# Product-key lookup and weight grids: eight heads per operation, four tokens per first one-hot, the weight in the second one-hot

## The chip, the cores and the metric

The kernel runs on one core of a Trainium2 chip. The metric is the device time of one execution in microseconds; three executions of the kernel before give a median of 4173.94 us (4171.84 to 4176.83). The engines are named as in the profile: PE is TensorE (PEld its weight loads), DVE is VectorE, ACT is ScalarE, POOL is GpSimd, SP is SyncE, which issues most DMAs.

## The reference, cut to what matters

Two transformer blocks follow each other on 256 tokens of 1024 features. The first has attention and a mixture of 32 experts (top 4, three 1024x1024 matrices for each expert). The second has two layers, each with a mixer and a PEER feed-forward part; it works on the 256 tokens and, in its first layer, on 256 context tokens as well. PEER is the part that the change touches:

```
def peer_ffn(h, w_q, sub_keys, u_tab, v_tab):
    # 8 heads, 2 x 128 sub-keys, top 16 per half -> 256 candidates -> top 16
    def one_block(xb):                                  # 128 tokens
        q = (xb @ w_q).reshape(128, 8, 2, 64)
        s = einsum('thpd,pkd->thpk', q, sub_keys)
        s1, i1 = top_k(s[:, :, 0], 16)
        s2, i2 = top_k(s[:, :, 1], 16)
        cand_s = s1[..., :, None] + s2[..., None, :]
        cand_i = i1[..., :, None] * 128 + i2[..., None, :]
        top_s, pos = top_k(cand_s, 16)                  # over the 256 candidates
        idx = take_along_axis(cand_i, pos)              # 0 .. 16383
        wts = softmax(top_s)
        act = gelu(einsum('thkd,td->thk', u_tab[idx], xb)) * wts
        return einsum('thk,thkd->td', act, v_tab[idx])
```

Each token thus picks 8 x 16 = 128 of 16384 experts, each with a weight.

## The kernel before

The kernel gathers nothing. For PEER it multiplies all 16384 rows of `u_tab` with the 256 tokens (**U**, L150 to L152, three products of high and low parts, into the banks `ps_u`), takes gelu, multiplies with a **grid** of weights (L880), and multiplies the result with all rows of `v_tab` (**V**, L897, L898, L900, into the banks `ps_a`). Both tables are read in chunks `wr` and split into `wh` (ACT, L117) and `wl` (DVE, L118). The grid holds for each token and each expert the sum of the weights that the token gives the expert: 128x128 numbers for a token, the two halves of the expert number being row and column.

PEER runs three times. Stage **B** is the context's, in layer 0; stage **A** the tokens' in layer 0; stage **C** the tokens' in layer 1. Each has a `peer_prep` that makes the grids and a `peer_pass` that makes U and V. In `peer_prep` there are two blocks of 128 tokens, and for each:

- `topk`: scores, top 16 and softmax. At its end stands the lookup (L746): for each of 8 heads and 16 picks one operation over the 50 candidates that can be among the top 16, with an accumulated sum, 128 in all. Then the numbers are split into two halves (L753 to L756), transposed together with the weights, and copied to `it` (L761, three rows of 128 tokens).
- `grid`: for each token a first one-hot `o1` on DVE (L788: iota equal to the first half, times the weight), a second one-hot `o2`, in one buffer for two tokens, and a matmul of the two (L789). Four tokens fill a bank of `ps_a`; ACT evicts it (L790) to `stg`, and 16 tokens are stored to DRAM (L792). Of eight `o2` buffers in a row POOL makes two (L778, `POOL_AT`); in the second block of tokens (`share` = 2) DVE makes four (L780); the others are ACT's, as the absolute difference (L782, one for each token) and then 1 minus it, clipped at zero, for both tokens at once (L784). So ACT makes six of eight in the first block of a stage, 48 in all, and two of eight in the second.

The order of instructions on each engine is fixed when the kernel is built, by a scheduler that keeps a timeline of its own with assumed durations: of the instructions whose inputs and buffers its timeline has ready it takes the next. How much of one stage stands between the instructions of another is so decided by assumed times. The buffers of each kind are counted: in stages A and C `o1` has 8 (one token each) and `o2` has 4 (two tokens each), in stage B they have 6 (`NB1`) and 3. A V cannot stand ahead of its stage's grids, while U can: in stages A and C the U of 40 pairs of chunks may run ahead.

Stage B is written as a filler of the first block's mixture of experts. The order interleaves it with that part's expert chunks, which are named by the matmuls of gate and up projection (L1055) and of down projection (L1089). I call eight rows of the order with them (16 matmuls in the trace, two loads `mo` of 1 MiB each) an expert chunk. A branch (`overflow`) is a barrier at 540 us of the trace; 192 expert chunks stand in all, 27 of them ahead of B's grids.

Of the kernel before, what the change touches and what calls it, by code (L numbers as in the profile page):

```python
# [10 lines left out]
F32 = mybir.dt.float32  # L11
# [3 lines left out]
AF = mybir.ActivationFunctionType  # L15
ALU = mybir.AluOpType
AX = mybir.AxisListType
# [3 lines left out]
P = 128  # L21
# [24 lines left out]
GP = 1  # L46
SPB = 4
PB = 8
NB1 = 6
POOL_AT = (1,5)  # L50
EL = (1, 3, 5, 7)
MOE_FIRST = 6
NCAND = sum(w for _, w in CAND) + 8
# [11 lines left out]
def kernel(ctx: ExitStack, tc: tile.TileContext, a: dict, out: bass.AP):  # L65
    nc = tc.nc
# [20 lines left out]
    def psum(tag):  # L87
        if tag == "g":
            tag = gtags[gnext[0] % len(gtags)]
            gnext[0] += 1  # L90
        return ps.tile([P, 512], F32, tag=tag, name="ps_" + tag, bufs=4 if tag == "a" else 2)
# [8 lines left out]
    ident, iota, lt_m, gt_m, ones_m = C("ident"), C("iota"), C("lt"), C("gt"), C("ones")  # L100
# [487 lines left out]
    for k2 in range(4):  # L588
        yb = ytr(k2)
        for c in range(2):  # L590
            k = 2 * k2 + c
# [105 lines left out]
    def topk(l, q, tk, idx, pt):  # L697
        keys, qT = q
        sc = []
        for tb in range(2):  # L700
# [39 lines left out]
            nc.vector.tensor_copy(tf, tx)  # L740
            ef = tk.tile([P, 8, 16], F32, tag="ef", name="ef")
            eqs = tk.tile([P, 8, 64], F32, tag="sc", name="eq", bufs=2)
            for h in range(8):
                for k in range(16):
                    eq = eqs[:, k % 8, 0:NCAND]
                    nc.vector.scalar_tensor_tensor(eq, iota[:, 0:NCAND], tf[:, h, k:k + 1], ce[:, h, :], op0=ALU.is_equal,  # L746
                                                   op1=ALU.mult, accum_out=ef[:, h, k:k + 1])
                if h % 2:
                    yield
            ei = tk.tile([P, P], I32, tag="ts", name="ei")  # L750
            e2 = tk.tile([P, P], I32, tag="tx", name="e2")
# [5 lines left out]
            tp = psum(pt)  # L757
            for i in range(3):
                nc.tensor.transpose(tp[:, i * P:(i + 1) * P], iw[i], ident)
            it = tk.tile([P, 3, P], F32, tag="it", name="it", bufs=2)  # L760
            nc.scalar.activation(it.rearrange("p c t -> p (c t)"), tp[:, :384], AF.Copy)  # L761
            idx.append(it)
            yield

    def grid(tk, it, gd, bufs, share):
        nstg, nb1, nb2 = bufs
        for tq in range(8):
            stg = tk.tile([P, P, 16], F32, tag="stg", name="stg", bufs=nstg)
            for t4 in range(4):
                bank = psum("a").rearrange("p (t i) -> p t i", t=4)  # L770
                for i2 in range(2):
                    o2q = tk.tile([P, 2, P], F32, tag="o2", name="o2", bufs=nb2)
                    on_pool = (2 * t4 + i2) in POOL_AT
                    on_dve = share and (2 * t4 + i2) % share == 0
                    for i in range(2):
                        t = tq * 16 + t4 * 4 + i2 * 2 + i
                        if on_pool:
                            nc.gpsimd.tensor_scalar(o2q[:, i, :], iota, it[:, 1, t:t + 1], None, op0=ALU.is_equal)  # L778
                        elif on_dve:
                            nc.vector.tensor_scalar(o2q[:, i, :], iota, it[:, 1, t:t + 1], None, op0=ALU.is_equal)  # L780
                        else:
                            nc.scalar.activation(o2q[:, i, :], iota, AF.Abs, bias=it[:, 1, t:t + 1], scale=-1.0)  # L782
                    if not on_dve and not on_pool:
                        nc.scalar.activation(o2q, o2q, AF.Relu, bias=1.0, scale=-1.0)  # L784
                    for i in range(2):
                        t = tq * 16 + t4 * 4 + i2 * 2 + i
                        o1 = tk.tile([P, P], F32, tag="o1", name="o1", bufs=nb1)
                        nc.vector.tensor_scalar(o1, iota, it[:, 0, t:t + 1], it[:, 2, t:t + 1], op0=ALU.is_equal, op1=ALU.mult)  # L788
                        nc.tensor.matmul(bank[:, 2 * i2 + i, :], o2q[:, i, :], o1, start=True, stop=True)  # L789
                nc.scalar.activation(stg[:, :, t4 * 4:t4 * 4 + 4].rearrange("p i t -> p t i"), bank, AF.Copy)  # L790
                yield
            STQ.dma_start(gd[:, tq], stg)  # L792

    def peer_prep(l, xm, tk, gd, bufs=(3, 8, 4), pt="g"):
        keys = tk.tile([P, P], F32, tag="keys", name="keys")
        nc.sync.dma_start(keys, a["p_keys"][l])
        qT = tk.tile([P, KD, T], F32, tag="stg", name="qT", bufs=bufs[0])

        def put_q(n, bank):
            nc.scalar.activation(qT[:, n:n + 2, :], bank, AF.Copy)  # L800

        gemm_nt(nt_src(a["p_w_q"][l]), xm, KD, put_q, pt=pt)
        yield
        idx = []
        tkg = topk(l, (keys, qT), tk, idx, pt)
        first = None
        for i, _ in enumerate(tkg):
            if len(idx) == 1 and first is None:
                first, at_ = grid(tk, idx[0], gd[0], bufs, 0), i
            if first is not None:  # L810
                drain(first, 1 if i - at_ < 5 else 4)
            yield
        drain(first)
        yield from grid(tk, idx[1], gd[1], bufs, 2)
# [374 lines left out]
    with filler():  # L1189
# [28 lines left out]
        cx_stack.close()  # L1218
        tkb_stack = ctx.enter_context(ExitStack())
        tkb = pool("tkb", stack=tkb_stack, side="right")  # L1220
        bprep = peer_prep(0, XB, tkb, gds[0], (2, NB1, 3), "u")
        drain(bprep, PB)
    overflow(mo, mres)
    general("g")
# [423 lines left out]
```

## Time and profile before

| | |
|---|---|
| median of three executions | 4173.94 us |
| the profiled execution, its own time | 4168.0 us |
| its span in the trace | 4166.2 us |
| mean granted clock of TensorE, as a share | 0.983 |
| PE busy | 4009.8 us, 96% |
| DVE busy | 2382.3 us, 57% |
| ACT busy | 1928.0 us, 46% |
| POOL busy | 166.6 us, 4% |

The shares are means over the span. The program has parts with different limits, so the windows below take them one by one: 545 to 820 us is from the barrier to B's first V, 820 to 2050 the rest of stage B with the experts, 2050 to 2250 the end of the experts, the normalisation and the mixer of the next layer, 2250 to 2321 the scores and the lookup of A's first block, 2321 to 2436 the grids of A's first block, 2436 to 2545 those of its second. Stage C repeats A's pattern from 3310 us on.

### The profile page before, as it was taken

To read this page: it belongs to the slowest core of one execution; us is meant where nothing else is said; L and a number is where in the kernel's file an instruction comes from. 1 tells how busy PE (TensorE), PEld (TensorE's weight loads), DVE (VectorE), ACT (ScalarE), POOL (GpSimd) and SP (SyncE) were. 2 spreads that over 40 slices of the span, in tenths; PEclk is the share of its full clock that TensorE was granted. 3 is DMA by queue.
4 is the path that set the end of the run, shared out by engine and by line. 5 is a ranking of instruction groups with operands and counts; after the bars stand their busy time and mean duration, and the time that the engine had idled before them with its cause. 6 is when DMAs were issued, how large, how long until landed. Compare 5 with 4: busy or idle time off the path is not lost.

```text
span 4166.2 us, 63176 instructions
## 1 busy us (share of the span) xinstructions
PE 4009.8 (96%) x23786; PEld 3059.7 (73%) x23786; DVE 2382.3 (57%) x6357; ACT 1928.0 (46%) x2835; POOL 166.6 (4%) x230
## 2 busy tenths in 40 slices
PE   8999979999999999999998999999998899999998
PEld 7676535566666666666587999788877699988887
DVE  4464596543333333333278997565455789766555
ACT  5543236533333333333243886345545349744443
POOL 0000001100000000000000120000000002200000
PEclk9999989999999999999999999999998899999999
DMA  7659869998988898998865578776774246787773
GB/s 258 239 190 359 324 254 338 358 340 322 341 324 337 321 348 319 337 341 329 321 211 167 205 260 318 257 238 215 259 257 149 94 159 229 260 291 242 234 238 126
DMA packets 340046, 1115.49 MB, mean 268 GB/s; under 512 B 28934, under 2 KB 128006, under 8 KB 283672
## 3 DMA queue, kind: packets, MB, share of 16 engines
q1 hardware_dynamic: 323896, 1043.22, 70.3%
q10 hardware_dynamic: 15552, 66.07, 4.0%
q8 instruction: 190, 3.11, 0.3%
q0 software_dynamic: 288, 2.10, 0.1%
q14 instruction: 120, 0.98, 0.1%
HBM read 1041.97 MB, written 69.30 MB: 267 GB/s over the span
## 4 chain that ended last, share of the span: by engine, by line
PE 72%; DVE 5%; ACT 2%; DMA 2%; issue 1%; POOL 0%; ACTq 0%; SPq 0%; DVEq 0%; POOLq 0%
PE ps_a L898 9%; PE ps_a L897 9%; PE ps_a L900 9%; PE ps_u L150 8%; PE ps_u L151 8%; PE ps_g L1055 8%; PE ps_u L152 8%; PE ps_g L1089 4%; PE ps_a L789 2%; PE ps_g L1101 1%; DVE wl L118 1%; PE ps_g L329 1%; PE ps_g L209 1%; PE ps_g L210 1%; PE ps_g L211 1%
## 5 line engine op out<-in xcount | busy, mean ns | idle before, releaser
L118 DVE TENSOR_TENSOR wl<-wr,wh 128x1024 fp32r<-128x1024 f32 x933 | 1131.6, 1220 | 1040.9 <-ACT wh L117 1025.4
L117 ACT ACTIVATE wh<-wr 128x1024 fp32r<-128x1024 f32 x933 | 979.8, 1055 | 1270.3 <-PE ps_u L151 500.1
L898 PE MATMUL ps_a<-wl,ah 128*128 128x512 f32 x1536 | 587.7, 398 | 3.1 <-DVE wl L118 3.1
L897 PE MATMUL ps_a<-wh,ah 128*128 128x512 f32 x1536 | 572.8, 397 | 0.0
L1055 PE MATMUL ps_g<-mo,xg 128*64 128x512 f32 x2048 | 474.5, 606 | 17.7 <-DMA mo<-in_w_gate_dram 11.5
L900 PE MATMUL ps_a<-wh,al 128*128 128x512 f32 x1536 | 479.7, 396 | 0.0
L897 PEld LDWEIGHTS ps_a<-wh,ah 128*128 128x128 f32 x1536 | 287.8, 188 | 79.1 <-issue 12.8
L898 PEld LDWEIGHTS ps_a<-wl,ah 128*128 128x128 f32 x1536 | 286.4, 188 | 76.1 <-issue 11.4
L900 PEld LDWEIGHTS ps_a<-wh,al 128*128 128x128 f32 x1536 | 287.1, 188 | 72.3 <-issue 6.8
L1055 PEld LDWEIGHTS ps_g<-mo,xg 128*64 128x64 f32 x2048 | 138.2, 138 | 272.2 <-issue 243.5
L150 PE MATMUL ps_u<-xbh,wh 128*128 128x256 f32 x1088 | 314.4, 289 | 1.0 <-ACT xbh L117 0.8
L151 PE MATMUL ps_u<-xbl,wh 128*128 128x256 f32 x1088 | 313.6, 288 | 0.5 <-DVE xbl L118 0.5
L152 PE MATMUL ps_u<-xbh,wl 128*128 128x256 f32 x1088 | 311.2, 286 | 0.0
L152 PE MATMUL ps_u<-xch,wl 128*128 128x256 f32 x960 | 274.1, 287 | 5.6 <-DVE wl L118 5.6
L150 PE MATMUL ps_u<-xah,wh 128*128 128x256 f32 x960 | 276.0, 288 | 2.8 <-ACT sp L859 2.7
L152 PE MATMUL ps_u<-xah,wl 128*128 128x256 f32 x960 | 273.9, 287 | 2.6 <-DVE wl L118 2.6
L151 PE MATMUL ps_u<-xal,wh 128*128 128x256 f32 x960 | 275.5, 287 | 0.0
L150 PE MATMUL ps_u<-xch,wh 128*128 128x256 f32 x960 | 274.5, 286 | 0.2 <-ACT wh L117 0.2
L151 PE MATMUL ps_u<-xcl,wh 128*128 128x256 f32 x960 | 274.5, 286 | 0.0
L788 DVE TENSOR_SCALAR o<-cst,it 128x128 f32<-128x128 f32 x768 | 232.2, 343 | 40.4 <-PE ps_a L789 39.6
L1089 PE MATMUL ps_g<-mo,hT 128*64 128x512 f32 x1024 | 238.7, 609 | 6.3 <-DMA mo<-in_w_down_dram 6.2
L789 PE MATMUL ps_a<-o,o 128*128 128x128 f32 x1536 | 226.9, 278 | 14.2 <-ACT o L784 10.1
(651 smaller groups left out, 6976.5 us busy)
## 6 DMA issues: line engine op xcount, KB each, us to landing
wr<-in_p_u_dram SPq DMA_DIRECT2D x384, 512.0 KB, 4.8
wr<-in_p_v_dram SPq DMA_DIRECT2D x384, 512.0 KB, 5.4
mo<-in_w_gate_dram SPq DMA_DIRECT2D x128, 1024.0 KB, 7.7
mo<-in_w_up_dram SPq DMA_DIRECT2D x128, 1024.0 KB, 7.2
mo<-in_w_down_dram SPq DMA_DIRECT2D x128, 1024.0 KB, 7.6
gd<-stg ACTq DMA_DIRECT2D x48, 1024.0 KB, 6.2
gr<-gd SPq DMA_DIRECT2D x96, 512.0 KB, 7.9
mw<-in_w_mod_dram SPq DMA_DIRECT2D x48, 512.0 KB, 5.1
```

What stands on the lines that cost most here:

```text
L117: nc.scalar.activation(h, src, AF.Copy)
L118: return nc.vector.tensor_sub(l, src, h.bitcast(F32)).ins
L150: nc.tensor.matmul(o, wh, xh, start=first, stop=False)
L151: nc.tensor.matmul(o, wh, xl, start=False, stop=False)
L152: nc.tensor.matmul(o, wl, xh, start=False, stop=last)
L788: nc.vector.tensor_scalar(o1, iota, it[:, 0, t:t + 1], it[:, 2, t:t + 1], op0=ALU.is_equal, op1=ALU.mult)
L789: nc.tensor.matmul(bank[:, 2 * i2 + i, :], o2q[:, i, :], o1, start=True, stop=True)
L897: nc.tensor.matmul(acc[tb][hf], ah[:, ts], wh[:, hs], start=first, stop=False)
L898: nc.tensor.matmul(acc[tb][hf], ah[:, ts], wl[:, hs], start=False, stop=False)
L900: nc.tensor.matmul(acc[tb][hf], al[:, ts], wh[:, hf * 512:(hf + 1) * 512], start=False, stop=fin)
L1055: nc.tensor.matmul(bank[64 * i:64 * i + 64, :], xg[:, kq * 4 + k, o:o + CAP], wt[i][:, k, :], start=(kq == 0 and k == 0), stop=False, skip ...
L1089: nc.tensor.matmul(bank[64 * i:64 * i + 64, :], hT[:, kq * 4 + k, 64 * i:64 * i + 64], wt[i][:, k, :], start=(kq == 0 and k == 0), stop=(k ...
```

## The change

The lookup becomes three operations for each of the 16 picks, over all eight heads at once (400 elements): iota equal to the pick, times the candidate's expert number, and a sum over each head. `o1` is made for four tokens at once and holds no weight. The weight goes into `o2`: on POOL and DVE as a second scalar of the same operation, on ACT as the scale and the bias of the second step, which is therefore issued for each token apart (two operations over 128 elements in place of one over 256). For the scale `it` gets a fourth row with the negative weights, by one more copy on ACT for each block. The buffers change too: `o1` has 3 in stages A and C and 2 in stage B, each now of four tokens; `o2` keeps 4 in stages A and C and has 2 in place of 3 in stage B.

```
-NB1 = 6
+NB1 = 2
...
             eqs = tk.tile([P, 8, 64], F32, tag="sc", name="eq", bufs=2)
-            for h in range(8):
-                for k in range(16):
-                    eq = eqs[:, k % 8, 0:NCAND]
-                    nc.vector.scalar_tensor_tensor(eq, iota[:, 0:NCAND], tf[:, h, k:k + 1], ce[:, h, :], op0=ALU.is_equal,
-                                                   op1=ALU.mult, accum_out=ef[:, h, k:k + 1])
-                if h % 2:
+            eq = eqs[:, :, 0:NCAND]
+            for k in range(16):
+                nc.vector.tensor_tensor(eq, iota[:, None, 0:NCAND].to_broadcast([P, 8, NCAND]), tf[:, :, k:k + 1].to_broadcast([P, 8, NCAND]),
+                                        op=ALU.is_equal)
+                nc.vector.tensor_mul(eq, eq, ce)
+                nc.vector.tensor_reduce(ef[:, :, k:k + 1], eq, axis=AX.X, op=ALU.add)
+                if k % 4 == 3:
                     yield
...
-            it = tk.tile([P, 3, P], F32, tag="it", name="it", bufs=2)
-            nc.scalar.activation(it.rearrange("p c t -> p (c t)"), tp[:, :384], AF.Copy)
+            it = tk.tile([P, 4, P], F32, tag="it", name="it", bufs=2)
+            nc.scalar.activation(it[:, 0:3, :].rearrange("p c t -> p (c t)"), tp[:, :384], AF.Copy)
+            nc.scalar.activation(it[:, 3, :], tp[:, 256:384], AF.Copy, scale=-1.0)
...
+                t0 = tq * 16 + t4 * 4
+                o1 = tk.tile([P, 4, P], F32, tag="o1", name="o1", bufs=nb1)
+                nc.vector.tensor_tensor(o1, iota[:, None, :].to_broadcast([P, 4, P]), it[:, 0, t0:t0 + 4, None].to_broadcast([P, 4, P]),
+                                        op=ALU.is_equal)
...
-                        if on_pool:
-                            nc.gpsimd.tensor_scalar(o2q[:, i, :], iota, it[:, 1, t:t + 1], None, op0=ALU.is_equal)
-                        elif on_dve:
-                            nc.vector.tensor_scalar(o2q[:, i, :], iota, it[:, 1, t:t + 1], None, op0=ALU.is_equal)
+                        if on_pool or on_dve:
+                            eng = nc.gpsimd if on_pool else nc.vector
+                            eng.tensor_scalar(o2, iota, it[:, 1, t:t + 1], it[:, 2, t:t + 1], op0=ALU.is_equal, op1=ALU.mult)
                         else:
-                            nc.scalar.activation(o2q[:, i, :], iota, AF.Abs, bias=it[:, 1, t:t + 1], scale=-1.0)
-                    if not on_dve and not on_pool:
-                        nc.scalar.activation(o2q, o2q, AF.Relu, bias=1.0, scale=-1.0)
+                            nc.scalar.activation(o2, iota, AF.Abs, bias=it[:, 1, t:t + 1], scale=-1.0)
+                            nc.scalar.activation(o2, o2, AF.Relu, bias=it[:, 2, t:t + 1], scale=it[:, 3, t:t + 1])
...
-                        o1 = tk.tile([P, P], F32, tag="o1", name="o1", bufs=nb1)
-                        nc.vector.tensor_scalar(o1, iota, it[:, 0, t:t + 1], it[:, 2, t:t + 1], op0=ALU.is_equal, op1=ALU.mult)
-                        nc.tensor.matmul(bank[:, 2 * i2 + i, :], o2q[:, i, :], o1, start=True, stop=True)
+                        nc.tensor.matmul(bank[:, 2 * i2 + i, :], o2q[:, i, :], o1[:, 2 * i2 + i, :], start=True, stop=True)
...
-    def peer_prep(l, xm, tk, gd, bufs=(3, 8, 4), pt="g"):
+    def peer_prep(l, xm, tk, gd, bufs=(3, 3, 4), pt="g"):
...
-        bprep = peer_prep(0, XB, tkb, gds[0], (2, NB1, 3), "u")
+        bprep = peer_prep(0, XB, tkb, gds[0], (2, NB1, 2), "u")

The order that the scheduler makes changes with it. First the PE's order in stage B, at a gap between two expert chunks. L1101 (after: L1103) puts an expert's result back on its tokens, L1055 (L1057) is an expert chunk, L789 (L791) a grid matmul of one token with its buffers `o2` and `o1`, L1058 (L1060) adds a bias. Before:

```order
L1101 MATMUL ps_g<-yo,pt 128x512
L1055 MATMUL ps_g<-mo,xg 64x512 x8
L789 MATMUL ps_a<-o_8840,o_8836 128x128
L789 MATMUL ps_a<-o_8843,o_8836 128x128
L789 MATMUL ps_a<-o_8854,o_8850 128x128
L789 MATMUL ps_a<-o_8857,o_8850 128x128
L789 MATMUL ps_a<-o_8863,o_8860 128x128
L789 MATMUL ps_a<-o_8866,o_8860 128x128
L1055 MATMUL ps_g<-mo,xg 64x512 x8
```

The same kind of place after the change:

```order
L1103 MATMUL ps_g<-yo,pt 128x512
L1057 MATMUL ps_g<-mo,xg 64x512 x8
L791 MATMUL ps_a<-o_8585,o_8594 128x128 x2
L791 MATMUL ps_a<-o_8605,o_8607 128x128 x2
L791 MATMUL ps_a<-o_8605,o_8614 128x128
L1057 MATMUL ps_g<-mo,xg 64x512 x8
L1060 MATMUL ps_g<-bgr,sel 128x512
L791 MATMUL ps_a<-o_8663,o_8665 128x128
L791 MATMUL ps_a<-o_8605,o_8614 128x128
L791 MATMUL ps_a<-o_8663,o_8665 128x128
L1057 MATMUL ps_g<-mo,xg 64x512 x8
```

Six tokens stood between two expert chunks, as many as three buffers `o2` hold; now mostly four stand there, or fewer. Counted over the whole order, 58 expert chunks stood ahead of B's first V, and now 74 do; ahead of the same V stood 335 matmuls of U, and now 317. All of B's work stands ahead of the next layer's mixer in both orders.

Second the ACT's order in the middle of the grids of A's first block. L782 and L784 (after: L788 and L789) are the two steps of `o2`, L790 (L792) evicts four tokens, L713 evicts scores of the second block; after the change L863 is a DMA that puts a product of U aside, L117 splits a table chunk and L794 stores a grid. Before:

```order
L782 ACTIVATE o_18390<-cst,it 128x128 x2
L790 ACTIVATE stg<-ps_a 128x4x128
L782 ACTIVATE o_18443<-cst,it 128x128 x2
L784 ACTIVATE o_18390<-o_18390 128x256
L790 ACTIVATE stg<-ps_a 128x4x128
L782 ACTIVATE o_18453<-cst,it 128x128 x2
L784 ACTIVATE o_18443<-o_18443 128x256
```

After:

```order
L789 ACTIVATE o_17916<-o_17916,it 128x128 x2
L788 ACTIVATE o_17954<-cst,it 128x128 x2
L792 ACTIVATE stg<-ps_a 128x4x128
L788 ACTIVATE o_17961<-cst,it 128x128 x2
L863 DMA sdr_6_19071<-sp 128x512
L117 ACTIVATE wh<-wr 128x1024
L789 ACTIVATE o_17954<-o_17954,it 128x128 x2
L794 DMA gd_2891<-stg 128x2048
L789 ACTIVATE o_17961<-o_17961,it 128x128 x2
```

The one step over 256 elements has become two over 128 that read `it`. Counted over the order, 600 matmuls of U stood between the first and the last grid of A's first block, and now 831 do; in the same stretch ACT splits 36 chunks in place of 27. 
## Rows read from the trace of the kernel before

**Rows 1.** The page: busy time of each engine, and GB/s in 40 slices.

```profile
PE 4009.8 (96%) x23786; PEld 3059.7 (73%) x23786; DVE 2382.3 (57%) x6357; ACT 1928.0 (46%) x2835; POOL 166.6 (4%) x230
...
GB/s 258 239 190 359 324 254 338 358 340 322 341 324 337 321 348 319 337 341 329 321 211 167 205 260 318 257 238 215 259 257 149 94 159 229 260 291 242 234 238 126
```

**Rows 2.** Windows: length, busy of PE, PEld, DVE, ACT, POOL, clock, DMA share, GB/s.

```profile
545.00:820.00 275.00, 244.57 (x1332) 136.13 (x1333) 189.75 (x1070) 146.66 (x306) 42.78 (x64) 0.96 0.88 330
820.00:2050.00 1230.00, 1230.00 (x6686) 795.41 (x6686) 464.23 (x579) 429.92 (x511) 0.00 (x0) 1.00 0.89 333
2050.00:2120.00 70.00, 64.61 (x341) 41.31 (x338) 30.73 (x46) 24.71 (x33) 1.12 (x2) 1.00 0.70 255
2120.00:2250.00 130.00, 115.17 (x693) 101.82 (x693) 96.03 (x176) 48.92 (x59) 8.07 (x7) 0.93 0.58 191
2250.00:2321.00 71.00, 68.48 (x493) 64.98 (x490) 66.31 (x441) 28.74 (x35) 0.00 (x0) 1.00 0.57 190
2321.00:2436.00 115.00, 110.31 (x934) 109.17 (x933) 112.87 (x583) 109.34 (x224) 23.68 (x32) 1.00 0.62 217
2436.00:2545.00 109.00, 109.00 (x930) 108.86 (x929) 85.41 (x274) 79.91 (x124) 23.92 (x32) 1.00 0.78 267
```

**Rows 3.** Waits of PE in 544 to 820 us, the two longest: us, times, longest.

```profile
PE ps_g L1055 <- DMA mo<-in_w_gate_dram: 6.8, 4, 4.3
PE ps_a L789 <- ACT o L784: 6.7, 9, 2.4
```

**Rows 4.** Groups by form, 820 to 2050 us: busy, mean ns, idle before.

```profile
L1055 PE MATMUL ps_g<-mo,xg 128*64 128x512 f32 x1374 | 313.8, 598 | 0.0
```

**Rows 5.** Timeline of PE in stage B: start, length, instructions.

```profile
639.45 1.60 PE L789 MATMUL ps_a<-o,o 128*128 128x128 f32 x12
640.98 3.65 PE L1055 MATMUL ps_g<-mo,xg 128*64 128x512 f32 x16
```

**Rows 6.** Groups by form, whole span, DVE.

```profile
L746 DVE SCALAR_TENSOR_TENSOR eq<-cst,tx,ce 128x50 f32<-128x50 f32 x768 | 160.7, 264 | 0.1
L788 DVE TENSOR_SCALAR o<-cst,it 128x128 f32<-128x128 f32 x768 | 232.2, 343 | 40.4 <-PE ps_a L789 39.6
L880 DVE TENSOR_TENSOR ge<-ge,gr 128x256 f32<-128x256 f32 x224 | 84.6, 420 | 33.6 <-ACT ge L859 32.2 <-DMA gr<-gd 1.3
L1067 DVE TENSOR_TENSOR gt<-gt,sg 128x512 f32<-128x512 f32 x32 | 22.1, 690 | 15.6 <-ACT sg L1064 15.5
```

**Rows 7.** Timeline of DVE in B's lookup and after it: start, length.

```profile
549.77 0.26 DVE L746 SCALAR_TENSOR_TENSOR eq<-cst,tx,ce 128x50 f32<-128x50 f32 x1
...
549.96 0.27 DVE L746 SCALAR_TENSOR_TENSOR eq<-cst,tx,ce 128x50 f32<-128x50 f32 x1
...
568.66 0.23 DVE L754 CAST iw<-e 128x128 f32<-128x128 int32 x1
568.92 0.23 DVE L755 TENSOR_SCALAR e<-ei 128x128 int32<-128x128 int32 x1
```

**Rows 8.** Groups by form, whole span, ACT.

```profile
L117 ACT ACTIVATE wh<-wr 128x1024 fp32r<-128x1024 f32 x927 | 975.6, 1057 | 1263.9 <-PE ps_u L151 497.0 <-PE ps_a L900 440.9 <-DMA wr<-in_p_u_dram 55.1
...
L782 ACT ACTIVATE o<-cst,it 128x128 f32<-128x128 f32 x384 | 126.7, 388 | 19.0 <-PE ps_a L789 18.9
L784 ACT ACTIVATE o<-o 128x256 f32<-128x256 f32 x192 | 76.3, 414 | 1.1
L1030 ACT ACTIVATE xg<-ps_g,lnc 128x256 f32<-128x256 f32 x64 | 32.2, 562 | 10.6 <-PE ps_g L1027 10.1
```

**Rows 9.** Timeline of ACT, two steps of one `o2` in A's first block.

```profile
2338.08 0.37 ACT L782 ACTIVATE o<-cst,it 128x128 f32<-128x128 f32 x1
...
2338.34 0.40 ACT L782 ACTIVATE o<-cst,it 128x128 f32<-128x128 f32 x1
```

More of the change, by code (lines that the diff above doesn't have):

```diff
@@ L775, in grid @@
                     for i in range(2):
-                        t = tq * 16 + t4 * 4 + i2 * 2 + i
-                        if on_pool:
-                            nc.gpsimd.tensor_scalar(o2q[:, i, :], iota, it[:, 1, t:t + 1], None, op0=ALU.is_equal)
-                        elif on_dve:
-                            nc.vector.tensor_scalar(o2q[:, i, :], iota, it[:, 1, t:t + 1], None, op0=ALU.is_equal)
-                        else:
-                            nc.scalar.activation(o2q[:, i, :], iota, AF.Abs, bias=it[:, 1, t:t + 1], scale=-1.0)
-                    if not on_dve and not on_pool:
-                        nc.scalar.activation(o2q, o2q, AF.Relu, bias=1.0, scale=-1.0)
+                        t = t0 + i2 * 2 + i
+                        o2 = o2q[:, i, :]
+                        if on_pool or on_dve:
+                            eng = nc.gpsimd if on_pool else nc.vector
+                            eng.tensor_scalar(o2, iota, it[:, 1, t:t + 1], it[:, 2, t:t + 1], op0=ALU.is_equal, op1=ALU.mult)
+                        else:
+                            nc.scalar.activation(o2, iota, AF.Abs, bias=it[:, 1, t:t + 1], scale=-1.0)
+                            nc.scalar.activation(o2, o2, AF.Relu, bias=it[:, 2, t:t + 1], scale=it[:, 3, t:t + 1])
                     for i in range(2):
-                        t = tq * 16 + t4 * 4 + i2 * 2 + i
-                        o1 = tk.tile([P, P], F32, tag="o1", name="o1", bufs=nb1)
-                        nc.vector.tensor_scalar(o1, iota, it[:, 0, t:t + 1], it[:, 2, t:t + 1], op0=ALU.is_equal, op1=ALU.mult)
-                        nc.tensor.matmul(bank[:, 2 * i2 + i, :], o2q[:, i, :], o1, start=True, stop=True)
+                        nc.tensor.matmul(bank[:, 2 * i2 + i, :], o2q[:, i, :], o1[:, 2 * i2 + i, :], start=True, stop=True)
                 nc.scalar.activation(stg[:, :, t4 * 4:t4 * 4 + 4].rearrange("p i t -> p t i"), bank, AF.Copy)
```

## The prediction

> **What bounds the kernel now.** I begin with the page: PE is busy 96% of the span, DVE 57%, ACT 46%, and the slices of GB/s reach 359 and not more [rows 1]. The change takes no matmul away, so it can save only time in which PE waits, or cost such time. Where that is, the windows show [rows 2], and the reader is to compare the first figure after the length, PE's busy time, with the length. From 545 to 820 us, where B's lookup and grids stand between expert chunks, PE has 244.6 of 275 us; it lacks 30, at 330 GB/s and a DMA share of 0.88. From 820 to 2050 it lacks nothing. From 2050 to 2250 it lacks 5.4 and 14.8 us. In A's lookup (2250 to 2321) it lacks 2.5, in the grids of A's first block (2321 to 2436) 4.7, in those of the second none. In that first block PE, DVE and ACT all stand near the limit: 110.3, 112.9 and 109.3 of 115 us. C, later, has the same code as A.
>
> Two views say what PE waits for in B's window. The waits name the load of an expert matrix and the second one-hot of ACT about equally, 6.8 and 6.7 us [rows 3]. The timeline shows why loads matter: an expert chunk starts 1.53 us after the 12 grid matmuls ahead of it (two for each of six tokens) [rows 5], and its own 16 matmuls take 16 x 313.8/1374 = 3.65 us [rows 4]. A chunk brings 2 x 1 MiB = 2.1 MB, so at that pace it would need 2.1 MB in 5.18 us, 405 GB/s, more than any slice has. Where chunks follow each other with only grids between them, the loads set the pace.
>
> **The change part by part.**
>
> *Lookup.* 128 operations that start 0.19 us apart [rows 7] take 24.3 us for a block. They become 48 operations over 400 elements. No row has that size; between 420 ns at 256 and 690 at 512 elements [rows 6] it is 572 ns. Operations that need nothing from each other overlap by some 0.08 us (0.19 apart against 0.264 long [rows 6, 7]); an operation that needs the one ahead of it starts 0.03 after its end (0.26 apart, 0.23 long [rows 7]). All three of a pick depend on each other. So 48 x 0.60 = 28.9 us, or 48 x 0.49 = 23.6 if other work of DVE always fills the gap: between -0.7 and +4.6 us for a block, and I take +4.6. The Trainium skill, "VectorE: DVE Perf Modes", section "The DRAIN you can't avoid", says that a semaphore between two operations of DVE costs nothing extra; by it the lookup would take 23.6 us. The rows speak against it. Behind the lookup on DVE stand the splits `wl`, and PE waits for the grids. What covers it in A is U, which runs ahead (PE has 68.5 of 71 us in that window [rows 2]), in B the expert chunks. So it costs nothing; without the cover it is 4.6 us for a first block, 14 for three.
>
> *First one-hot.* Four operations of 232.2/768 = 0.302 us each, 1.21, become one over 512 elements, 0.69 by the row of that form [rows 6]: 0.52 less for four tokens, 32 x 0.52 = 16.6 us less of DVE for a block. The first matmul of four now waits for 0.69 in place of 0.34, with 8 or 12 tokens of `o1` buffered against it. The rows show that at 128 elements most of the 343 ns is not paid by element. The Trainium skill, "VectorE: DVE Perf Modes", section "The perf-mode tier table", has fp32 `tensor_scalar` at twice the rate of `tensor_tensor`; by rate alone, an estimate from its 1227 and 2293 ns for 2048 elements, four tokens would go from 0.31 to 0.57 us, DVE in A's first block would need 8.6 us more, 121.5 of 115, and the sum would be 13 us higher for A and C. The row of 690 ns against four of 343 speaks against it.
>
> *Second one-hot.* On ACT 414 ns for two tokens become two operations that read two pointers. Their price lies between 388 ns (L782, 128 elements, one pointer) and 562 (L1030, 256 elements, two) [rows 8]; I take 475, the middle. One more start overlaps by some 0.1 (0.26 apart, 0.37 long [rows 9]). So 2 x 0.475 - 0.414 - 0.1 = +0.44 us for a buffer (bounds +0.26 and +0.61), and for the 48 buffers of a first block +21 us (+12 to +29). POOL's operation gains a second scalar; no row has its form. Between nothing and a doubling POOL reaches 48 of 109 us [rows 2], still hidden. DVE's `o2` in second blocks takes the form of L788, 0.30 us, where DVE has 85 of 109 us [rows 2]. The extra copy to `it` is one ACT operation under 0.42 us for a block, hidden in ACT's idle time; uncovered, 2.5 us in all six blocks.
>
> *The order, stage B.* Two buffers `o2` in place of three let fewer tokens stand between two chunks. By the order 16 more expert chunks stand ahead of the first V. They bring 16 x 2.1 = 33.6 MB into a window that moved 275 us x 330 GB/s = 90.8 MB [rows 2]. 124.4 MB take 377 us at 330 GB/s and 346.5 at 359: the window grows by 71.5 to 102 us. The window after it, where PE lacks nothing, gets the same PE work back: 16 x 3.65 = 58.5 us of chunks [rows 4], some 61 other matmuls of these experts (gathers, biases, returns, counted over the two orders) at the window's mean of 1230/6686 = 0.184 us [rows 2], 11 us, less 18 matmuls of U, which come later now, at 109/930 = 0.117 [rows 2], 2 us: 67.5. B costs +4 to +34.5, and I take the middle, +19: this window waited for ACT as well as for loads, so that part of the 330 is not the loads' own limit. At the end of the experts (2050 to 2120) more U and V are left to fill PE's 5.4 idle us: -4 (-5 to 0). They stand ahead of the next layer's mixer in both orders, so they don't fill the 14.8 after it.
>
> *The order, stages A and C.* The scheduler puts 831 U where 600 stood: 231 x 0.117 = 27 us more PE work, 137 in all. ACT there goes from 109.3 by +21 (second one-hots) and by nine more splits at 1.06 us [rows 8], 9, to 139, beside PE 137. The U are not new; they lack later. What counts is PE's idle time, now 4.7 us. With ACT no longer behind PE I take +3 for the stage. Bounds: -5, if DVE's relief lets all of the idle go, and +9.5, with the dear pointer (ACT 147 against 137, less 4.7, and a little for the later wait). A and C together +6 (-10 to +19).
>
> **Sum.** +19 - 4 + 6 = +21 us. The profiled execution took 4168.0, so 4189; it lies 5.9 us under the median, so 4195 beside 4173.94. The bounds added up are -11 and +53.
>
> **The rivals.** A difference under 0.2% (8.3 us) is about what a measurement of this kernel can't tell from none.
>
> *Faster: DVE is what holds the grids.* For it: DVE has the most busy time of all in A's first block, 112.9 of 115 [rows 2], and loses 16.6 there. Then PE's 4.7 idle us and the like in C go (-10), the tail gives -5, and the loads in B run at the best slice's rate (+4): -11, 4163. It decides if ACT's two Relus take under 0.40 us each, so that ACT stays below PE. Against it: the waits name ACT as the maker that PE waits for [rows 3], and ACT gets more work. 0.15.
>
> *Slower than my sum: loads stay at 330 GB/s and ACT becomes A's and C's bound.* +34.5 + 19 = +53, 4227. For it: ACT has 109 of 115 already; against it: slices of 359 exist [rows 1]. 0.20.
>
> *No measurable change.* The moved chunks cost only their floor, ACT and PE stay level: +4 - 4 + 6 = +6, 4180. For it: all that moves is work that must be done anyway, and PE is full for 1230 us after it. Against it: the tail is the only idle time that the moved work can fill, 5.4 us. 0.21.
>
> **How the numbers follow.** My forecast, 4183 to 4210 as its own range, has 0.44. Slower by over 0.2% are it and the second rival: 0.64. Same: the third, 0.21. Faster: 0.15. The range goes from the faster rival's 4164 to 4230, a little past the slower rival.
>
> **What the next profile would show.** Right: B's first V some 85 us later than 818, with loads named first among PE's waits; DVE's busy time some 80 us lower in all (six blocks of 16.6, less six lookups of up to 4.6); ACT's second step near 475 ns; ACT's busy share in A's first block level with PE's. Wrong: PE idle in that window no longer than 30 us although it is longer (the loads had room: then the first or third rival); o1 above 0.8 us for four tokens; waits of PE for `o2` in A and C that were not there (second rival). What I can't price is whether the scheduler's assumed times fit the new operations: if they are too short, every engine queue is in the wrong order at once, and the slower rival comes true in all three stages.

## The result and the profile after

The changed kernel takes 4217.78 us (median of four, 4209.51 to 4221.92) beside 4172.89 for the kernel before: a ratio of 1.0104, 95% interval 1.0086 to 1.0121, 45 us slower. The forecast was 4195, slower, with a range of 4164 to 4230. The profiled execution took 4209.5 us, the least of the four, so the trace shows 41.5 of the 45 us against [rows 1]'s execution.

The page of the changed kernel, its first part and GB/s by slice:

```profile
PE 4029.1 (96%) x23786; PEld 3068.9 (73%) x23786; DVE 2323.3 (55%) x4533; ACT 2007.2 (48%) x3029; POOL 262.9 (6%) x230
...
GB/s 255 240 198 364 300 286 315 318 335 331 344 336 341 323 348 309 338 326 343 255 216 157 211 245 304 249 259 212 262 257 151 108 166 214 262 290 232 242 235 128
```

DVE lost 59 us and POOL gained 96, and neither is near the limit. PE made the same 23786 matmuls and is busy 19 us more. Where, the windows say; the columns are those of [rows 2], the cuts are moved to the same events (the first V of B is at 934.8 us, and was at 818.5):

```profile
545.00:934.80 389.80, 332.93 (x1629) 165.40 (x1630) 185.55 (x522) 188.17 (x388) 67.79 (x64) 0.94 0.85 321
934.80:2050.00 1115.20, 1115.20 (x6067) 721.33 (x6067) 419.25 (x522) 389.53 (x461) 0.00 (x0) 1.00 0.89 334
2050.00:2161.90 111.90, 111.90 (x672) 94.58 (x669) 69.11 (x91) 52.00 (x63) 1.13 (x2) 1.00 0.60 196
2290.00:2369.00 79.00, 78.25 (x576) 74.79 (x575) 71.62 (x237) 33.83 (x41) 0.00 (x0) 1.00 0.61 198
2369.00:2508.00 139.00, 138.74 (x1165) 137.30 (x1166) 119.39 (x344) 138.94 (x287) 43.13 (x34) 1.00 0.65 222
2508.00:2584.00 76.00, 75.37 (x647) 75.17 (x647) 55.08 (x108) 71.33 (x123) 35.90 (x30) 1.00 0.76 273
```

The window with B's grids has grown by 116 us, and PE lacks 56.9 us in it where it lacked 30.4 [rows 2]. After it PE lacks nothing up to the last V of B; the 5.4 idle us of the tail are gone. In A's grids PE and ACT are both full, 138.7 and 138.9 of 139 us, and PE's idle 4.7 us [rows 2] are gone as well. The whole of stage B, from the barrier to its last V, first before and then after the change:

```profile
545.00:2122.50 1577.50, 1541.68 (x8363) 974.89 (x8364) 687.21 (x1700) 602.36 (x852) 43.90 (x66) 0.99 0.88 329
```

```profile
545.00:2161.90 1616.90, 1560.03 (x8363) 981.31 (x8364) 673.90 (x1134) 629.70 (x912) 68.91 (x66) 0.99 0.86 322
```

The same 8363 matmuls take 39.4 us longer: 21.0 us more in which PE is idle (56.9 against 35.8), and 18.4 us more in which it is busy. All that follows B, to the end, adds 2 us. So the time went in B, and within B in the window of the grids. Where the busy time went, the groups by form of the whole stage say in part: the 512 matmuls of the grids are busy 12.8 us longer than before (first row before, second after). Groups overlap in time, so they are no full split of the 18.4.

```profile
L789 PE MATMUL ps_a<-o,o 128*128 128x128 f32 x512 | 72.4, 286 | 10.8 <-ACT o L784 6.7 <-DVE o L788 2.5 <-DVE o L780 1.2
```

```profile
L791 PE MATMUL ps_a<-o,o 128*128 128x128 f32 x512 | 85.2, 299 | 29.4 <-POOL o L786 14.1 <-DVE o L786 9.4 <-ACT o L789 5.3
```

PE's waits in the window of the grids, after the change (us, times, longest):

```profile
PE ps_a L791 <- POOL o L786: 14.1, 17, 1.6
PE ps_g L1057 <- DMA mo<-in_w_gate_dram: 10.7, 5, 3.8
PE ps_g L1057 <- DMA mo<-in_w_up_dram: 9.8, 6, 2.9
PE ps_a L791 <- DVE o L786: 9.4, 13, 1.1
PE ps_a L791 <- ACT o L789: 5.3, 6, 2.3
PE ps_g L1091 <- DMA mo<-in_w_down_dram: 3.9, 3, 2.1
```

28.8 us are waits for a second one-hot, of whichever engine made it, and 24.4 for loads. Before the change all lines of the same view gave 10.4 us for one-hots, of both kinds, and 15.5 for loads; [rows 3] shows its two longest. Part of the 18 us of longer busy time is the clock. Windows of 20 us in the changed kernel; the third figure from the end is the granted clock:

```profile
745.00:765.00 20.00, 14.63 (x69) 6.22 (x67) 3.29 (x5) 9.59 (x23) 2.60 (x2) 0.93 0.90 339
765.00:785.00 20.00, 16.77 (x68) 7.90 (x65) 4.78 (x11) 6.76 (x14) 4.22 (x4) 0.76 0.52 201
785.00:805.00 20.00, 16.65 (x88) 8.26 (x87) 7.34 (x18) 9.21 (x18) 4.64 (x4) 1.00 0.98 365
```

PE had worked 14.6 of 20 us when the mean clock of the next 20 fell to 0.76, about half of that stretch at the lower of the two levels (1.2 GHz); 68 matmuls, not all of one size, took as long there as 88 in the next. Over the window the clock is 0.94, and was 0.96 over a shorter one [rows 2]: 6% of 390 us against 4% of 275. By these means, an estimate, the clock is some 12 of the 18 us; no view names the other 6.

The new operations themselves (groups by form: busy, mean ns, idle before):

```profile
L786 POOL TENSOR_SCALAR o<-cst,it 128x128 f32<-128x128 f32 x192 | 235.3, 1233 | 848.4 <-PE ps_a L791 460.5 <-ACT it L762 222.1 <-DVE m L687 122.9
...
L789 ACT ACTIVATE o<-o,it 128x128 f32<-128x128 f32 x384 | 173.4, 520 | 0.0
L788 ACT ACTIVATE o<-cst,it 128x128 f32<-128x128 f32 x384 | 135.5, 424 | 24.5 <-PE ps_a L791 23.7 <-ACT stg L792 0.4
L775 DVE TENSOR_TENSOR o<-cst,it 128x512 f32<-128x512 f32 x192 | 132.6, 693 | 106.8 <-PE ps_a L791 104.6 <-ACT it L762 2.0
...
L786 DVE TENSOR_SCALAR o<-cst,it 128x128 f32<-128x128 f32 x192 | 59.9, 354 | 0.0
...
L747 DVE TENSOR_TENSOR eq<-eq,ce 128x400 f32<-128x400 f32 x96 | 55.9, 583 | 1.9
L745 DVE TENSOR_TENSOR eq<-cst,tx 128x400 f32<-128x400 f32 x96 | 55.4, 577 | 2.1
L748 DVE TENSOR_REDUCE ef<-eq 128x8 f32<-128x400 f32 x96 | 54.6, 568 | 1.8
```

### The profile page after: what moved, and what is told of

The parts are those of the page before. It is cut to its first block, busy times and chain, and to the rows that moved or that the text cites. A ratio compares the mean times of both kernels' runs of the same rounds, so it can differ in the third digit from the quotient of the medians.

```text
span 4207.7 us, 61328 instructions
## 1 busy us (share of the span) xinstructions
PE 4029.1 (96%) x23786; PEld 3068.9 (73%) x23786; DVE 2323.3 (55%) x4533; ACT 2007.2 (48%) x3029; POOL 262.9 (6%) x230
## 4 chain that ended last, share of the span: by engine, by line
PE 70%; ACT 6%; DMA 5%; DVE 5%; issue 1%; POOL 0%; SPq 0%; ACTq 0%; DVEq 0%; POOLq 0%
PE ps_g L1057 9%; PE ps_a L900 8%; PE ps_a L899 8%; PE ps_a L902 8%; PE ps_u L150 7%; PE ps_u L151 7%; PE ps_u L152 7%; PE ps_g L1091 5%; PE ps_a L791 3%; ACT wh L117 2%; DVE wl L118 1%; ACT o L789 1%; DMA mo<-in_w_up_dram 1%; PE ps_g L1103 1%; ACT stg L792 1%
## 5 line engine op out<-in xcount | busy, mean ns | idle before, releaser
L117 ACT ACTIVATE wh<-wr 128x1024 fp32r<-128x1024 f32 x933 | 988.4, 1062 | 1248.9 <-PE ps_u L151 495.0
L900 PE MATMUL ps_a<-wl,ah 128*128 128x512 f32 x1536 | 587.7, 398 | 4.3 <-DVE wl L118 4.2
L1057 PE MATMUL ps_g<-mo,xg 128*64 128x512 f32 x2048 | 482.0, 614 | 25.9 <-DMA mo<-in_w_gate_dram 15.5
L899 PEld LDWEIGHTS ps_a<-wh,ah 128*128 128x128 f32 x1536 | 288.9, 189 | 88.5 <-ACT wh L117 13.3
L1057 PEld LDWEIGHTS ps_g<-mo,xg 128*64 128x64 f32 x2048 | 139.9, 140 | 286.8 <-issue 248.2
L900 PEld LDWEIGHTS ps_a<-wl,ah 128*128 128x128 f32 x1536 | 288.1, 189 | 78.1 <-issue 12.3
L151 PE MATMUL ps_u<-xbl,wh 128*128 128x256 f32 x1088 | 313.2, 288 | 0.5 <-DVE xbl L118 0.5
L786 POOL TENSOR_SCALAR o<-cst,it 128x128 f32<-128x128 f32 x192 | 235.3, 1233 | 848.4 <-PE ps_a L791 460.5
L151 PE MATMUL ps_u<-xal,wh 128*128 128x256 f32 x960 | 276.0, 287 | 0.0
L151 PE MATMUL ps_u<-xcl,wh 128*128 128x256 f32 x960 | 274.6, 286 | 0.0
L791 PE MATMUL ps_a<-o,o 128*128 128x128 f32 x1536 | 241.0, 283 | 30.9 <-POOL o L786 14.4
L791 PEld LDWEIGHTS ps_a<-o,o 128*128 128x128 f32 x1536 | 205.4, 192 | 62.6 <-POOL o L786 19.8
```

The source lines that it names most:

```text
L117: nc.scalar.activation(h, src, AF.Copy)
L151: nc.tensor.matmul(o, wh, xl, start=False, stop=False)
L786: eng.tensor_scalar(o2, iota, it[:, 1, t:t + 1], it[:, 2, t:t + 1], op0=ALU.is_equal, op1=ALU.mult)
L791: nc.tensor.matmul(bank[:, 2 * i2 + i, :], o2q[:, i, :], o1[:, 2 * i2 + i, :], start=True, stop=True)
L899: nc.tensor.matmul(acc[tb][hf], ah[:, ts], wh[:, hs], start=first, stop=False)
L900: nc.tensor.matmul(acc[tb][hf], ah[:, ts], wl[:, hs], start=False, stop=False)
```

## The experiments

**Theory 1**: the lost third buffer `o2` stretches B's grids over more expert chunks, in a window where PE is idle and its clock low; each microsecond that the window grows costs a part of itself. **Theory 2**: POOL's dearer operation holds the grids. Four kernels ran first, on one chip, beside the kernel before (4168.8 us there).

*A third buffer for the changed kernel.* Cut to the lines that change. Only the last line gives the buffer; the others make its room.

```
-ts_ = tk.tile([P, 8, 16], F32, tag="ts", name="ts")
+ts_ = iw[1].rearrange("p (h k) -> p h k", h=8)
-ef = tk.tile([P, 8, 16], F32, tag="ef", name="ef")
+ef = iw[0].rearrange("p (h k) -> p h k", h=8)
-ei = tk.tile([P, P], I32, tag="ts", name="ei")
+ei = iw[1].bitcast(I32)
-bprep = peer_prep(0, XB, tkb, gds[0], (2, NB1, 2), "u")
+bprep = peer_prep(0, XB, tkb, gds[0], (2, NB1, 3), "u")
```

> The changed kernel with three o2 buffers in stage B in place of two; the room comes from three small tiles of the lookup that now share others' space, nothing else changes. In the order the first V of B stands after 63 expert chunks (58 before, 74 after the change). Theory 1 (the lost buffer stretches the grids over 16 more expert chunks, and loads and a low clock make each of them dear): 4180 to 4192 us, since 5 of 16 chunks are left, about 12 of the 45 us. Theory 2 (the two-scalar operation on POOL, 1233 ns against 735, holds the grids, whatever the buffers): 4203 or more, PE still waits over 20 us for POOL.

Measured: 4169.65 us, ratio to the kernel before 0.9998 (0.9989 to 1.0008). The whole 45 us are gone, more than theory 1 asked for: its numbers are missed too, on the other side from theory 2's. The window with the grids, cut at its first V, and its waits for one-hots:

```profile
545.00:853.70 308.70, 271.85 (x1449) 147.90 (x1447) 181.80 (x533) 182.98 (x384) 65.78 (x64) 0.95 0.90 337
```

```profile
PE ps_a L791 <- ACT o L789: 9.1, 8, 3.1
...
PE ps_a L791 <- POOL o L786: 4.8, 7, 1.7
```

PE lacks 36.9 us instead of 56.9, and POOL, at the same price, is waited for 4.8 us instead of 14.1. This trace is of the slowest of ten executions (4179.4 us), and what stands ahead of B's window came 7 us later in it, so a start at 545 us makes the window look 7 us too long. Counted from the same event, the first gather of tokens behind the barrier (before: `537.55 0.58 PE L1026`, at 544.45 in this run), B's stage up to its last V is as long as before the change, first before and then here:

```profile
537.55:2122.50 1584.95, 1548.71 (x8395) 981.55 (x8396) 694.66 (x1768) 606.20 (x859) 43.90 (x66) 0.99 0.88 329
```

```profile
544.45:2129.70 1585.25, 1547.95 (x8397) 982.19 (x8398) 677.90 (x1163) 633.46 (x924) 67.02 (x66) 0.99 0.88 329
```

*The kernel before with two buffers.*

```
-bprep = peer_prep(0, XB, tkb, gds[0], (2, NB1, 3), "u")
+bprep = peer_prep(0, XB, tkb, gds[0], (2, NB1, 2), "u")
```

> The kernel before with two o2 buffers in stage B in place of three, nothing else. The first V of B stands after 68 expert chunks. Theory 1: 4190 to 4205 us, 10 of 16 chunks, some 25 us more than before. Theory 2: under 4181, no change that can be measured, since POOL has its old operation.

Measured: 4194.56 us, 1.0054 (1.0041 to 1.0067), 26 us slower, inside theory 1's numbers. So the buffer alone, with the old operations, is about half of the loss. No run makes the room of the kernel above without giving the buffer; this one shows the buffer from the other side, with no other edit.

*POOL out of stage B.* DVE makes POOL's two of eight there.

```
-eng = nc.gpsimd if on_pool else nc.vector
+eng = nc.gpsimd if on_pool and nb1 != NB1 else nc.vector
```

> The changed kernel with POOL's o2 of stage B made on DVE, two buffers as in the changed kernel. The first V of B stands after 72 chunks. Theory 1: 4203 to 4215 us, 14 of 16 chunks are left and only the waits for POOL go, 14 us at most. Theory 2: 4175 to 4195.

Measured: 4206.39 us, 1.0091 (1.0067 to 1.0115). The window and its longest waits:

```profile
545.00:920.30 375.30, 318.50 (x1604) 162.49 (x1604) 201.68 (x597) 186.20 (x387) 0.00 (x0) 0.95 0.87 330
```

```profile
PE ps_a L791 <- ACT o L789: 15.7, 15, 3.5
PE ps_g L1057 <- DMA mo<-in_w_gate_dram: 14.2, 6, 4.1
PE ps_g L1091 <- DMA mo<-in_w_down_dram: 11.6, 5, 5.0
PE ps_a L791 <- DVE o L786: 7.5, 17, 0.9
```

PE still lacks 56.8 us. The wait for POOL has not gone; it has moved to ACT and to the loads. The engine that a wait names was the last to be ready here, and taking it out gave PE no time back.

*POOL's second scalar in the kernel before.*

```
-nc.gpsimd.tensor_scalar(o2q[:, i, :], iota, it[:, 1, t:t + 1], None, op0=ALU.is_equal)
+nc.gpsimd.tensor_scalar(o2q[:, i, :], iota, it[:, 1, t:t + 1], iota[:, 1:2], op0=ALU.is_equal, op1=ALU.mult)
```

> The kernel before with a second scalar operand in POOL's operation (the product with a column of iota that holds ones), so that POOL takes some 1233 ns for each and the result is the same; everything else as before, three buffers. The first V of B stands after 60 chunks. Theory 1: 4172 to 4182 us, three buffers cover it. Theory 2: 4187 or more.

Measured: 4169.09 us, 0.9991 (0.9979 to 1.0002). This is a little under theory 1's range too. POOL's operation took 1033 ns here, less than in the changed kernel, and nothing was lost. Theory 2 falls on all four runs. What POOL's price costs with two buffers is not told apart: the kernel without POOL in B has 1.0091, the changed one 1.0104, and the intervals overlap.

```profile
L778 POOL TENSOR_SCALAR o<-cst,it 128x128 f32<-128x128 f32 x192 | 197.0, 1033 | 763.7 <-PE ps_a L789 382.6 <-ACT it L761 370.9 <-ACT o L782 8.5
```

Four more kernels, on another chip (before: 4170.15), asked whether a fourth buffer gives more, what the lookup costs alone, and whether it is the loads that make the window dear.

*Four buffers.* The room is made as above, and by an `o1` for two tokens at a time with three buffers in stage B:

```
+w1 = 2 if nstg == 2 else 4
+for j in range(0, 4, w1):
+    o1 = tk.tile([P, w1, P], F32, tag="o1", name="o1", bufs=nb1)
...
-bprep = peer_prep(0, XB, tkb, gds[0], (2, NB1, 2), "u")
+bprep = peer_prep(0, XB, tkb, gds[0], (2, 3, 4), "u")
```

> The changed kernel with four o2 buffers in stage B; to make room o1 is there made for two tokens at a time with three buffers, and three small tiles of the lookup share others' space. The first V of B stands after 58 chunks, as before the change. Theory 1 (the number of o2 buffers sets how long the grids take in B, and only that costs): no slower than the kernel before, 4158 to 4172 us. Rival (ACT's dearer second step costs in all three stages, and the third buffer hid it by chance): 4175 or more.

Measured: 4167.24 us, 0.9996 (0.9985 to 1.0006): no slower, and no faster either than with three.

*The lookup alone*, in the kernel before; the edit is the lookup's part of the change, as shown above:

> The kernel before with the new lookup alone. The first V of B stands after 58 chunks, as before. Theory 1: no change that can be measured, 4163 to 4176 us: lookups of 26 to 29 us a block are hidden by U and expert chunks. Rival (the three dependent operations of a pick hold up the first grids): three first blocks by 4.6 us, 4180 or more.

Measured: 4186.22 us, 1.0037 (1.0023 to 1.0051), 16 us slower. My forecast of nothing is wrong, and the rival's time is right. The trace is of the slowest of five executions (4191.2 us, 23 over the trace before). Of the 23 us 3.8 lie ahead of the first gather behind the barrier, 2.8 between it and B's last V, 13.0 from there to A's last V and 3.5 behind that. PE's waits from 2575 to 4175 us:

```profile
PE ps_a L898 <- ACT wh L117: 12.1, 5, 5.0
...
PE ps_a L899 <- DVE wl L118: 5.4, 2, 2.7
```

Before the change V waited for no `wh` in those stages, and 3.1 us for `wl`:

```profile
PE ps_a L898 <- DVE wl L118: 3.1, 2, 1.5
```

With the longer lookup the order puts 192 matmuls of U more ahead of A's first V (1769 against 1577 up to the last grid), and the splits for V are late when it starts. The first of these waits in the timeline of PE:

```profile
2579.98 2.08 PE L898 MATMUL ps_a<-wh,ah 128*128 128x512 f32 x4 [5.00 <-ACT wh L117]
2584.76 1.22 PE L899 MATMUL ps_a<-wl,ah 128*128 128x512 f32 x2 [2.71 <-DVE wl L118]
```

The clock over these 25 us is 0.80, and was 1.00 at A's first V before the change, an estimated 5 us more:

```profile
2575.00:2600.00 25.00, 16.58 (x59) 12.41 (x60) 20.27 (x41) 10.74 (x13) 0.00 (x0) 0.80 1.09 358
```

So most of what A lost lies at its first V, and not at the first grids, where the rival had it. That the longer order of U is what makes the splits late is argued: no run changes the one without the other.

*Half loads*, in the kernel before and in the changed one. Half of each expert tile is left out, and the other half used twice:

```
-ins = nc.sync.dma_start(w_.rearrange("p k f -> p (k f)"), src).ins
+ins = nc.sync.dma_start(w_[:, 0:2, :].rearrange("p k f -> p (k f)"), src[:, 0:1024]).ins
...
-wt[i][:, k, :]
+wt[i][:, k % 2, :]
```

> The kernel before with half of the bytes of every expert matrix: each load brings half of its tile, and the matmuls use that half twice, so that the output is not the reference's; all matmuls stay. Made to be compared with the next run. The scheduler lets more chunks pass: the first V of B stands after 83. Both theories: 4110 to 4165 us, the 15 us of waits for loads go, and what lies ahead of the barrier gains too.

> The changed kernel with the same half loads (output not the reference's). The first V of B stands after 102 chunks, 19 more than in the run with half loads and the kernel before. If loads are what makes the extra chunks dear (the step of my prediction): less than 15 us above that run. If it is the grids' own waits for o2 and what they do to the clock: 30 us or more above it.

Measured: 4132.47 and 4166.14 us, 0.9916 (0.9899 to 0.9932) and 0.9996 (0.9985 to 1.0006) of the kernel before: 33.7 us between them. So with half the bytes three quarters of the 45 us are still there (in the traces 28 us of it up to B's last V). The windows up to B's first V, before and changed:

```profile
545.00:898.80 353.80, 332.24 (x1781) 166.05 (x1777) 220.57 (x1242) 158.28 (x328) 41.74 (x64) 1.00 0.69 229
```

```profile
545.00:1012.90 467.90, 428.03 (x2164) 201.72 (x2161) 217.08 (x655) 200.48 (x412) 64.72 (x64) 0.98 0.65 216
```

216 GB/s is far below what the core moved in other windows (334, 339 and 365 GB/s above), and PE still lacks 39.9 us in the changed kernel, 21.6 in the other. So the loads' mean rate is not what makes the longer window dear. But the time above 30 us that I had asked for came without the cause that I had named with it. The scheduler, seeing shorter loads, put chunks closer, and PE waited for loads 25.1 us in the changed one and 10.4 in the other; for one-hots it waited 5.0 us and 2.4:

```profile
PE ps_g L1091 <- DMA mo<-in_w_down_dram: 11.7, 7, 2.7
PE ps_g L1057 <- DMA mo<-in_w_up_dram: 10.1, 9, 3.6
PE ps_a L791 <- ACT o L789: 4.7, 5, 1.5
```

That single loads come late at a mean rate with room to spare is left as a rival. A run with more than the four buffers that the expert tiles have would test it; there is none.

The last four kernels asked whether a version beats both (before on that chip: 4169.06).

*The one-hots with the old lookup*, with four, three and two buffers:

> The run with four o2 buffers, with the old lookup: the one-hot part of the change alone, with room for it. The first V of B stands after 57 chunks. If the parts add up (lookup +15 us alone, so the one-hots are worth -15): 4148 to 4161 us. Rival (the lookup only costs where DVE also makes the old first one-hots; with the new ones DVE has room for it): 4162 to 4172, the same as with the new lookup.

Measured: 4167.23 us, 0.9995 (0.9986 to 1.0004).

> The run with the third o2 buffer, with the old lookup. The first V of B stands after 61 chunks. If the parts add up: 4150 to 4163 us. Rival as above: 4165 to 4175.

Measured: 4165.69 us, 0.9990 (0.9980 to 0.9999).

> The changed kernel with the old lookup, two o2 buffers. The first V of B stands after 74 chunks, as in the changed kernel. If the parts add up: 15 us under the changed kernel, 4195 to 4206 us. Rival (the lookup costs nothing here): 4210 to 4220.

Measured: 4206.47 us, 1.0092 (1.0077 to 1.0107).

The parts do not add up. The new lookup costs 0.37% beside the old one-hots, and beside the new ones too little to measure: with three buffers 0.9998 against 0.9990, with two 1.0104 against 1.0092. The rival expectation holds with four and with three buffers; with two the time lies between the two expectations, half a us above the one for parts that add up, and decides nothing.

*DVE makes two of eight second one-hots in the first blocks too*, with four buffers and the old lookup:

```
-first, at_ = grid(tk, idx[0], gd[0], bufs, 0), i
+first, at_ = grid(tk, idx[0], gd[0], bufs, 4), i
```

> The same, and in the first block of each stage DVE makes two of eight o2 that were ACT's. The first V of A comes after about 95 fewer matmuls of U. If ACT bounds the grids of A and C and falls behind with the splits at the first V (12 us of waits in both): 4140 to 4155 us. Rival (PE is busy all through those grids, nothing to gain): as the run before, within 4 us.

Measured: 4161.91 us, 0.9985 (0.9976 to 0.9994), the lowest median, 7 us under the kernel before and less than the 0.2% that I called measurable; its interval overlaps that of the one-hots with three buffers. Neither expectation holds: it is 5 us under the one-hots with four buffers, where the rival allowed 4. The waits at A's first V that it was to remove were small in that run already (1.8 us), so why it gains is open.

## Why the prediction came out as it did

*Right:* slower, within the range. That the range held the time is in part luck: 4217.8 lies above the 4183 to 4210 that the forecast gave itself, and the range went up to 4230 for the slower rival. The operations on DVE came as the rows said: 568 to 583 ns for a lookup's operation (572 predicted), 693 for the first one-hot (690). The bytes of B's window were right too, 389.8 us x 321 GB/s = 125 MB (124.4 predicted), and so was the work that the later window got back: 1231.5 us from the first V to 2050 became 1115.2, and with the tail the stretch to the last V shrank by 76.9 (67.5 and the tail's 4 predicted). In A's first block ACT and PE stand level at 139 us, as worked out (139 and 137); A and C with all between them cost 2 us (6 predicted), though not as worked out: the idle time of the grids went, and V waited 13.3 us for its splits where it had waited 3.1.

```profile
PE ps_a L899 <- ACT wh L117: 9.1, 5, 3.4
...
PE ps_a L900 <- DVE wl L118: 4.2, 2, 2.4
```

*Too small:* the term of B's window. I had it grow by 71.5 to 102 us and took the middle; it grew by 116. The step that failed is the price by the loads' rate: "loads set the pace", with 330 to 359 GB/s as the bounds. The rate went down, to 321, with half the bytes three quarters of the loss stayed, and loads were not named first among PE's waits, as the signs had it: one-hots were, in sum. In place of the loads it is the third buffer `o2` that decides. In the table the window runs from the first gather behind the barrier to B's first V; that gather came 0.6 to 8.0 us later in the other traces than in the one before, which a start at 545 us would count as B's. From it every kernel has the same 8395 matmuls up to B's last V (two records more in two of the traces). Each line is one traced execution.

| kernel | `o2` in B | chunks ahead of first V | window, us | PE idle in it, us | B's last V against before, us |
|---|---|---|---|---|---|
| DVE share, old lookup | 4 | 56 | 264 | 25 | -2.1 |
| four buffers, changed | 4 | 58 | 274 | 28 | -3.4 |
| four buffers, old lookup | 4 | 57 | 275 | 32 | +0.6 |
| before | 3 | 58 | 281 | 31 | 0 |
| before, new lookup | 3 | 58 | 282 | 35 | +2.8 |
| before, POOL two scalars | 3 | 60 | 293 | 38 | -1.4 |
| three buffers, old lookup | 3 | 61 | 303 | 37 | +1.5 |
| three buffers, changed | 3 | 63 | 309 | 37 | +0.3 |
| before, two buffers | 2 | 68 | 358 | 48 | +28.5 |
| changed, no POOL in B | 2 | 72 | 377 | 57 | +29.6 |
| changed | 2 | 74 | 397 | 58 | +38.8 |
| two buffers, old lookup | 2 | 74 | 404 | 64 | +43.1 |

So the cost is not a fixed part of each microsecond by which the window grows. With three or four buffers windows of 264 to 309 us cost nothing beyond 3 us, whichever operations fill them; with two buffers windows of 358 to 404 cost 28 to 43. Why it breaks between three and two buffers no run shows. What the cost consists of, the changed kernel's trace shows: the longer window takes PE's work from a stretch where PE lacks nothing into one where it loses time. PE's idle time in the window grew by 26.5 us, of which the tail gave 5.4 back, and the busy time of the same matmuls by 18.4, together the 39.4 us of B. The prediction has no term for the longer busy time, and so none for the clock, and it took the idle time from the loads. That 68 chunks become 74 with the new operations is the order's doing; that it comes from their assumed times was argued, not tried.

*Wrong, without weight in the sum:* DVE's busy time fell by 59 us, not by some 80. The first one-hots gave the 99.6 us foreseen; the six lookups took some 20 back, and DVE's own second one-hots, which the 80 left out, 13 (46.9 to 59.9 us). POOL between nothing and a doubling "still hidden": it took 1233 against 735 ns and was waited for 14 us, but without it others were waited for in its place. ACT's second step took 520 ns, not 475, within the bounds.

*Wrong, and hidden by another part:* the lookup at nothing. Alone it costs 16 us. A price near it, 14 us for three uncovered first blocks, stood in the text, but that it is near is chance: the cover that I named (U runs ahead) did its work in A, and the loss came behind it, where V waits for its splits. Beside the new one-hots the lookup costs nothing that can be measured. That this is due to the first one-hots, which take 17 us a block off DVE, no run shows by itself.

*The rivals:* the slower one came nearest in time (4227). One half of its sum, +34.5 us for B, was nearer to the 39.4 than my 19; the other, +19 for ACT as the bound of A and C, is not there. That 19 was not worked out either: ACT's 10 us over PE less the 4.7 give 5 for a stage, not 9.5. The faster one was right that the grids of A and C lose their idle time (4.7 us to 0.3 in A's first block); that DVE's relief did it is not shown, since the order also put more U there. Of that nothing reached the end, since V then waited for its splits. What I held against this rival, [rows 3], are waits of B's window and say nothing of A.

The two answers to what a dependent operation of DVE costs were 0.49 and 0.60 us from start to start. The second was drawn from a pair in [rows 7] where the later operation overwrites what the earlier one reads; here each reads what the one ahead wrote. The timeline of the changed lookup shows 0.61, at a length of 0.57 to 0.58:

```profile
542.87 0.57 DVE L745 TENSOR_TENSOR eq<-cst,tx 128x400 f32<-128x400 f32 x1
543.48 0.58 DVE L747 TENSOR_TENSOR eq<-eq,ce 128x400 f32<-128x400 f32 x1
544.09 0.57 DVE L748 TENSOR_REDUCE ef<-eq 128x8 f32<-128x400 f32 x1
```

The rule of the Trainium skill that the prediction weighed there ("VectorE: DVE Perf Modes", section "The DRAIN you can't avoid": a semaphore between two operations costs nothing extra) would have given 0.49; the measurement decides for 0.61.

## What to carry to other kernels

Ask of each buffer that an edit gives up what stands between its uses: here one buffer of 1 KB a partition, given up for operations that saved DVE 59 us it didn't lack, cost 45 us, because a fixed order then spread one stage over 74 pieces of another in place of 58. Giving the buffer back took the loss away at 63 pieces. Price such a spreading by what PE loses in that stretch, idle time and longer busy time together, not by the resource that its waits name: here POOL, taken out, left the wait as long. And cut two traces at the same event, not at the same time. And a part that is hidden may be hidden by something that has its own price: the lookup alone cost 16 us.

## What had not been expected of the hardware

A second scalar operand on POOL took a 128x128 operation from 735 to 1233 ns; with the operand from another tile it took 1033. On DVE it went from 289 to 354 ns for the same shape, near the price of the old first one-hot (343 [rows 6]). The two forms before:

```profile
L778 POOL TENSOR_SCALAR o<-cst,it 128x128 f32<-128x128 f32 x192 | 139.2, 735 | 806.2 <-PE ps_a L789 409.6 <-ACT it L761 373.6 <-ACT yo L1092 12.3
...
L780 DVE TENSOR_SCALAR o<-cst,it 128x128 f32<-128x128 f32 x192 | 46.9, 289 | 0.4 <-PE ps_a L789 0.4
```

On ACT two pointer operands at 128 elements cost 520 ns, more than the 414 of 256 elements without them [rows 8].
